# A hybrid decoder layer on one core: the experts' rows in slot order, loaded by plain transfers; four fp32 chunks per expert; a moved output norm

## The chip, the cores and the metric

The kernel runs on one core of a Trainium2 chip. The metric is the device time of one execution in microseconds. It was measured three times for the kernel before: median 2206.45 us, from 2205.89 to 2207.40. The profile below is of a further execution.

## The reference

One layer over 2048 tokens of width 1024, all fp32: a mixer (retention in four heads beside a gated short convolution), then a hierarchical mixture of 64 experts, then a last norm.

```python
def mixer(h, w_in, ret_gn_w, conv_w, w_o):
    proj = h @ w_in                                   # 1024 -> 3584
    ...
    return jnp.concatenate([ret, conv], axis=-1) @ w_o

def hier_moe(h, rg_w, rg_b, re_w, re_b, w_gate, w_up, w_down):
    ...
    p_group, g_sel = lax.top_k(g_prob, 1)             # one group of 8
    ...
    top_p, top_i = lax.top_k(e_prob, TOP_K)           # 2 of the group's 8 experts
    gate = p_group[:, None] * (top_p / jnp.sum(top_p, axis=-1, keepdims=True))
    # every token's row goes through its two experts:
    #   y += gate * (silu(x @ w_gate[e]) * (x @ w_up[e])) @ w_down[e]
    ...

x = x + mixer(rmsnorm(x, norm1_w), ...)
x = x + hier_moe(rmsnorm(x, norm2_w), ...)
return rmsnorm(x, final_norm_w)
```

An expert has 1024 x 512 weights for gate and for up and 512 x 1024 for down, 6 MB in fp32. A token's two experts belong to the same group. The kernel gives each expert 96 slots; what does not fit goes through a loop at the end, which these inputs don't need for more than a check of the count.

## The kernel before

**Dense stage.** The sequence goes in four blocks of 512 tokens. For each block the kernel projects the input (`w_in`), runs retention and convolution and projects back (`w_o`). Weight pieces come into the buffer `wraw` and are split by ScalarE and VectorE into a high and a low part, so that a product of fp32 accuracy is three fast matmuls (`hi hi`, `hi lo`, `lo hi`). A matmul on unsplit fp32 data is called an fp32 chunk here; it shows as two records of the same matmul. A table of steps (`at(step, function, ...)`) sets where the smaller work of a block stands between the matmuls.

**Routing.** For each tile of 128 tokens of a block: `turn_rows` adds the squares and takes the reciprocal root (GpSimd, `rr`, L455), and stores the residual rows to the output; `norm_rows` makes h and stores it to `h_rows` in the order of tokens; `logits`, `choose`, `rank1`, `rank2`, `gates` and `spread` (L592) find each token's experts, its rank among the expert's tokens and the entries of a table that holds for each expert and slot the token's number. `address` and `record` write the same entries to a list in memory by indirect stores from GpSimd (L573). In the last block the table is built on chip (`place`), since the first expert waits for it, and the tiles' routing goes one after another between the last matmuls of `w_o`.

**Experts.** `estream` lists the work: for each q the eight chunks of gate and the eight of up of expert q, then the eight steps of down of expert q-1 (`wi` is 0, 1, 2 for gate, up, down; `c` is the chunk). The pieces of that loop that matter here:

- `load_unit` (L631): SP loads weights in units of 1 MB, six to an expert, into 17 buffers, each as soon as its buffer's last reader is done. SP issues in program order. Each transfer also waits for the one eight before it: in the program's listing, `DMAHW0` to `DMAHW7` are the counters of SP's transfers in rotation, and `DMASW0` to `DMASW7` those of GpSimd's.
- `split_hi` (ScalarE, L671) and `split_lo` (VectorE, L677) split two chunks at once, a piece, LEAD = 5 pieces ahead of the matmuls. `plain(w, c)` (L656) names the chunks that are not split: two of eight of gate and of up, four of eight of down, eight per expert in all. So eight pieces per expert are split.
- `gather(q + 3)` (L698) at the first chunk of gate: GpSimd fetches the 96 rows of h of expert q+3 from `h_rows` by an indirect transfer; a slot without a token has an index out of bounds and moves nothing. `xpose` (L720 to L727) transposes them on TensorE and splits six of eight chunks into `xhi` and `xlo`; two remain whole.
- `regather(q + 1)` (L705) then fetches the rows of the residual stream, from the output in memory, into the same buffer. A buffer `row` or `pair` thus holds first h, then the residual row, to which `add_rows` adds the expert's weighted product.
- `hpose` (L751) transposes the hidden rows of expert q-1, which `up_act` has written as [k, p].
- For the experts of the later half of each token's pair (`later`), `norm1_rows` squares the finished rows in two halves (ScalarE) at chunk 4 of gate, `norm2_rows` scales them (L789, L792) at chunk 4 of up, and `put_rows` (L820) stores them to the output by an indirect transfer. The first eight experts are stored without the norm.

Before each indirect transfer GpSimd writes a `spacer`.

Of the kernel before, what the change touches and what calls it, by code (L numbers as in the profile page):

```python
# [79 lines left out]
def hybrid_layer(ctx: ExitStack, tc: tile.TileContext, x, xT, norm1, w_in, gn_w, conv_w, w_o, norm2, norm2r,  # L80
# [4 lines left out]
    h_d = nc.dram_tensor("h_rows", (S, D), F32, kind="Internal").ap()  # L85
    list_d = nc.dram_tensor("slots", (RANKS * NE, 4), F32, kind="Internal").ap()
# [386 lines left out]
    def norm_rows(b, i, eng, to=None):  # L473
        t = x2t[i]
        to = t if to is None else to
        r2 = rt["r2"][:, i:i + 1]
        if eng is dve:
            dve.scalar_tensor_tensor(to, t, r2, n2b, op0=OP.mult, op1=OP.mult)
        else:
            act.activation(to, t, AF.Copy, scale=r2)  # L480
            pool.tensor_tensor(to, to, n2b, op=OP.mult)
        r0 = b * C + i * P
        sp.dma_start(h_d[r0:r0 + P, :], to)

# [80 lines left out]
    def address(b, i):  # L565
        c = rt["c", i]
        dve.scalar_tensor_tensor(c["slot"], c["rk"], float(NE), c["e"], op0=OP.mult, op1=OP.add)

# [87 lines left out]
    def plain(w, c):  # L656
        return c >= (4 if w == 2 else 6)
# [34 lines left out]

    def gather(q):
        if q >= NE:
            return
        e = order[q]
        spaced()
# [12 lines left out]
    NX, NH = 6, 2  # L710


    def xpose(q):
        g, w = row_of(q), EX["work"]
        hi, lo = (w.tile([P, NX, CAP], F32R, name="x" + n) for n in ("hi", "lo"))
        whole = w.tile([P, KD - NX, CAP], F32, name="xwhole")
        for k0 in (0, 4):
            p = bank("pxg")
            for j in range(4):
                pe.transpose(p[:, j * P:j * P + CAP], g[:, k0 + j::KD], ident[:CAP, :CAP])  # L720
            pv = p.rearrange("p (k t) -> p k t", k=4)[:, :, :CAP]
            n = min(4, NX - k0)
            ks = slice(k0, k0 + n)
            act.activation(hi[:, ks], pv[:, :n], AF.Copy)  # L724
            dve.tensor_tensor(lo[:, ks], pv[:, :n], hi[:, ks].bitcast(F32), op=OP.subtract)  # L725
            if n < 4:
                act.activation(whole, pv[:, n:], AF.Copy)  # L727
        EX["xT", q] = hi, lo, whole
# [7 lines left out]
    def gate_act(q, p):  # L736
        sg = EX["work"].tile([CAP, FF], F32, name="sg")
# [3 lines left out]
    def up_act(q, p):  # L741
        h = EX["work"].tile([CAP, KF, P], F32, name="hrow")
        dve.tensor_tensor(h.rearrange("t k p -> t p k"), p.rearrange("t (p k) -> t p k", k=KF),
                          EX["sg", q].rearrange("t (p k) -> t p k", k=KF), op=OP.mult)
        EX["h", q] = h

    def hpose(q):
        w = EX["work"]
        p = bank("ph")
        for k in range(KF):  # L750
            pe.transpose(p[:, k * P:k * P + CAP], EX["h", q][:, k], ident[:CAP, :CAP])  # L751
# [3 lines left out]
        pv = p.rearrange("p (k t) -> p k t", k=KF)[:, :, :CAP]  # L755
        act.activation(hi, pv[:, :n], AF.Copy)
        dve.tensor_tensor(lo, pv[:, :n], hi.bitcast(F32), op=OP.subtract)
        act.activation(whole, pv[:, n:], AF.Copy)
# [8 lines left out]
    def add_rows(q, ys):  # L767
        r = row_of(q)
        EX["s", q] = EX["work"].tile([CAP, 3], F32, name="osum", bufs=2)
# [5 lines left out]
    def norm1_rows(q):  # L775
        e, sums, r = order[q], EX["s", q], row_of(q)
# [58 lines left out]
    at(12, prep_consts)  # L835
    for b in range(NB):
# [31 lines left out]
        if b < NB - 1:  # L868
# [5 lines left out]
            for i in range(TB):  # L874
# [7 lines left out]
                at(so + 2 * i + 7, address, b, i)  # L882
                at(so + 2 * i + 7, record, b, i)
# [45 lines left out]
    for m in range(TB):  # L929
        for n, s in enumerate(rest):  # L930
# [7 lines left out]
            else:  # L938
# [75 lines left out]
    dve.tensor_scalar(nsec, sec, -1.0, 1.0, op0=OP.mult, op1=OP.add)  # L1014
    for i in range(TB):
# [7 lines left out]
    for i, (q, wi, c) in enumerate(estream):  # L1023
# [7 lines left out]
        if i in (36, 40, 44):  # L1031
            two = pair(FIRST[i // 4 - 9])
            if i < 44:
                EX["rows"] += two
                for j in (2, 1):
                    clear(len(EX["rows"]) - j)
                    if i == 36:
                        gather(5 - j)
# [17 lines left out]
        if wi < 2:  # L1056
# [12 lines left out]
            if wi == 1 and c == 4 and later(q - 2):  # L1069
                norm2_rows(q - 2)  # L1070
                put_rows(q - 2)
            if c == 7:
# [4 lines left out]
                else:  # L1077
# [4 lines left out]
                    else:  # L1082
                        weights(q - 1)
                        weights(q, EX["fw"])
        else:
# [4 lines left out]
            if q < NE - 1:  # L1090
                if c == 7:
# [122 lines left out]
```

## Time and profile before

| | |
|---|---|
| median of 3 runs | 2206.45 us |
| the profiled execution's own time | 2207.35 us |
| its span (first to last instruction) | 2205.5 us |
| TensorE busy | 2154.6 us, 98% |
| VectorE busy | 1417.4 us, 64% |
| ScalarE busy | 1127.9 us, 51% |
| GpSimd busy | 768.8 us, 35% |
| mean DMA rate | 262 GB/s |

Shares of busy time are means over stages: up to about 930 us the dense stage runs, from 944 us on the experts. In the profile PE is TensorE, DVE VectorE, ACT ScalarE, POOL GpSimd and SP the engine that issues plain transfers. "DMA share" is the mean busy share of the core's 16 DMA engines, q1 the queue of plain transfers, q0 that of indirect ones. Matmul records overlap, so the pace of matmuls is read from their starts. A row of SP's timeline with xN stands for N issues one behind the other, from the first one's start to the last one's end, waits between them included.

### The profile page before, as it was taken

What the parts mean: (1) busy time and instruction counts of PE and PEld (TensorE: products, weight loads), DVE (VectorE), ACT (ScalarE), POOL (GpSimd) and SP (SyncE); (2) the same over time, 40 slices, a digit from 0 to 9 for tenths busy, and PEclk for the clock granted to TensorE, in tenths of its full rate; (3) what the DMA queues carried; (4) which work ended last, traced back from release to release, by engine and by line L of the source; (5) the groups of instructions that cost most, each with busy time, mean ns of one, the idle gap of its engine ahead of it and who ended that gap; (6) DMA issues with size and microseconds to landing.
All of it is one profiled execution on the core that took longest, in us unless ns stands there. A gap on an engine that the chain in (4) does not pass through costs nothing. (4 is left out here: it accounts for less than half of the span.)

```text
span 2205.5 us, 27810 instructions
## 1 busy us (share of the span) xinstructions
PE 2154.6 (98%) x9417; PEld 1505.9 (68%) x9418; DVE 1417.4 (64%) x2265; ACT 1127.9 (51%) x1927; POOL 768.8 (35%) x982
## 2 busy tenths in 40 slices
PE   8999999999999999799999999999999999999998
PEld 6888888888888888655656656656555555555554
DVE  4667566657566666666666666666666665666665
ACT  4324342443343323555556666666655665566564
POOL 0010031002200120331234444445555655565556
PEclk9999999999999999899999999999999999999999
DMA  8335344524453446679999999999999999999994
GB/s 263 108 112 177 95 141 129 167 92 153 123 164 96 134 155 241 229 247 370 363 360 361 360 364 359 353 352 363 357 354 347 356 354 354 358 357 358 357 359 154
DMA packets 136099, 578.69 MB, mean 262 GB/s; under 512 B 23440, under 2 KB 23792, under 8 KB 86736
## 3 DMA queue, kind: packets, MB, share of 16 engines
q1 hardware_dynamic: 113424, 526.43, 67.9%
q0 software_dynamic: 22528, 50.44, 7.2%
q8 instruction: 75, 1.23, 0.2%
q14 instruction: 72, 0.59, 0.1%
HBM read 559.94 MB, written 44.20 MB: 274 GB/s over the span
## 5 line engine op out<-in xcount | busy, mean ns | idle before, releaser
L677 DVE TENSOR_TENSOR ring<-unit,ring 128x1024 fp32r<-128x1024 f32 x342 | 411.7, 1230 | 230.7 <-ACT ring L671 225.3
L671 ACT ACTIVATE ring<-unit 128x1024 fp32r<-128x1024 f32 x342 | 346.0, 1051 | 190.6 <-DMA unit<-in_w_gate_dram 105.5
L291 PE MATMUL acc<-hhi,ring 128*128 128x512 f32 x1280 | 404.9, 393 | 8.5 <-ACT ring L166 5.6
L167 DVE TENSOR_TENSOR ring<-wraw,ring 128x512 fp32r<-128x512 f32 x256 | 172.6, 687 | 185.0 <-ACT ring L166 185.0
L166 ACT ACTIVATE ring<-wraw 128x512 fp32r<-128x512 f32 x256 | 153.7, 625 | 265.2 <-issue 111.0
L291 PEld LDWEIGHTS acc<-hhi,ring 128*128 128x128 f32 x1280 | 241.6, 189 | 58.3 <-ACT ring L166 5.3
L677 DVE TENSOR_TENSOR part<-unit,part 128x1024 fp32r<-128x1024 f32 x170 | 206.3, 1229 | 112.8 <-ACT part L671 111.5
L291 PE MATMUL acc<-hlo,ring 128*128 128x512 f32 x640 | 250.2, 391 | 0.0
L1052 PE MATMUL acc<-unit,xwhole 128*96 128x512 f32 x512 | 240.4, 592 | 0.0
L1052 PE MATMUL acc<-unit,ewhole 128*96 128x512 f32 x512 | 230.3, 592 | 0.0
L671 ACT ACTIVATE part<-unit 128x1024 fp32r<-128x1024 f32 x170 | 173.7, 1051 | 93.5 <-DMA unit<-in_w_gate_dram 50.4
L732 PE MATMUL acc<-ring,xhi 128*96 128x512 f32 x512 | 217.5, 425 | 2.7 <-ACT xhi L724 2.4
L734 PE MATMUL acc<-ring,xlo 128*96 128x512 f32 x512 | 202.9, 396 | 7.1 <-DVE xlo L725 7.1
L733 PE MATMUL acc<-ring,xhi 128*96 128x512 f32 x512 | 202.5, 396 | 0.0
L291 PE MATMUL acc<-ring,mix 128*128 128x512 f32 x768 | 185.4, 396 | 0.0
L291 PE MATMUL acc<-ring,hhi 128*128 128x512 f32 x512 | 162.2, 398 | 0.0
L291 PEld LDWEIGHTS acc<-ring,mix 128*128 128x128 f32 x768 | 142.6, 189 | 28.6
L1052 PEld LDWEIGHTS acc<-unit,ewhole 128*96 128x96 f32 x512 | 83.3, 163 | 110.7 <-issue 101.6
L764 POOL TENSOR_SCALAR pair<-pair,sec,nsec 96x1024 f32<-96x1024 f32 x56 | 147.3, 2630 | 2.6
L1052 PEld LDWEIGHTS acc<-unit,xwhole 128*96 128x96 f32 x512 | 83.1, 162 | 86.1 <-issue 68.1
L792 POOL TENSOR_TENSOR pair<-pair 96x1024 f32<-96x1024 f32 x31 | 77.9, 2513 | 182.3 <-ACT pair L789 182.2
L291 PEld LDWEIGHTS acc<-hlo,ring 128*128 128x128 f32 x640 | 121.1, 189 | 24.2
(233 smaller groups left out, 3641.8 us busy)
## 6 DMA issues: line engine op xcount, KB each, us to landing
unit<-in_w_down_dram SPq DMA_DIRECT2D x128, 1024.0 KB
unit<-in_w_gate_dram SPq DMA_DIRECT2D x128, 1024.0 KB
unit<-in_w_up_dram SPq DMA_DIRECT2D x128, 1024.0 KB
wraw<-in_w_in_dram SPq DMA_DIRECT2D x225, 256.0 KB
wraw<-in_w_o_dram SPq DMA_DIRECT2D x64, 256.0 KB
xs<-in_x_dram SPq DMA_DIRECT2D x16, 512.0 KB
x<-in_x_dram SPq DMA_DIRECT2D x16, 512.0 KB
out_dram<-x SPq DMA_DIRECT2D x16, 512.0 KB
```

What stands on the lines that cost most here:

```text
L166: act.activation(hi, src, AF.Copy)
L167: dve.tensor_tensor(lo, src, hi.bitcast(F32), op=OP.subtract)
L291: pe.matmul(o, l, r, start=first and j == 0, stop=last and j == 2)
L671: act.activation(t[:, 0], src, AF.Copy)
L677: dve.tensor_tensor(lo, src, hi.bitcast(F32), op=OP.subtract)
L732: pe.matmul(o, ahi, whi, start=first, stop=False)
L733: pe.matmul(o, ahi, wlo, start=False, stop=False)
L734: pe.matmul(o, alo, whi, start=False, stop=last)
L764: pool.tensor_scalar(m, EX["fw"], EX["sec"][:, e:e + 1], EX["nsec"][:, e:e + 1], op0=OP.mult, op1=OP.add)
L792: pool.tensor_tensor(r, r, m, op=OP.mult)
L1052: pe.matmul(o, whole[:, k - hi.shape[1]], wt, start=False, stop=last)
```

## The change

1. **Rows in slot order.** A second array `h_slots` holds h in the order of expert and slot, 64 x 96 rows. 48 plain transfers fill it with zeros during the dense stage (`fill_slots`). For each tile, `sort_rows` writes its 128 rows of h there by two indirect stores from GpSimd (each token has two experts); `address` computes the slots on VectorE. From expert 3 on `gather` is one plain transfer of 96 rows, issued by SP; `clear` of those row buffers is dropped.
2. **Four fp32 chunks.** `plain` is now true only for the last four steps of w_down. All chunks of gate and up are split, ten pieces per expert, and `xpose` splits all eight chunks of x.
3. **Hidden rows.** `up_act` writes h as it comes; the transposes read it with a stride.
4. **Output norm.** `norm1_rows` squares all 1024 columns at once, so the GpSimd addition goes; `norm2_rows` and `put_rows` move from chunk 4 of up of expert q to chunk 4 of down of expert q-1, eight chunks later.

```diff
+    hs_d = nc.dram_tensor("h_slots", (NE * CAP, D), F32, kind="Internal").ap()
...
+    def fill_slots(i):
+        sp.dma_start(hs_d[i * P:(i + 1) * P], empty[:P * D // 4].rearrange("(p n) w -> p (n w)", p=P))
...
     def address(b, i):
...
+        dve.tensor_scalar(far, c["rk"], float(CAP), float(NONE), op0=OP.is_ge, op1=OP.mult)
+        dve.tensor_tensor(far, far, c["rk"], op=OP.add)
+        dve.scalar_tensor_tensor(hs, c["e"], float(CAP), far, op0=OP.mult, op1=OP.add)
...
+    def sort_rows(b, i):
+        c = rt["c", i]
+        for j in range(2):
+            pool.memset(spacer, 0.0)
+            s_ = pool.indirect_dma_start(
+                out=hs_d, out_offset=bass.IndirectOffsetOnAxis(ap=c["hslot"][:, j:j + 1], axis=0),
+                in_=c["h"], in_offset=None, bounds_check=NE * CAP - 1, oob_is_err=False)
...
     def plain(w, c):
-        return c >= (4 if w == 2 else 6)
+        return w == 2 and c >= 4
...
     def gather(q):
...
+        if q >= 3:
+            sp.dma_start(row_of(q), hs_d[e * CAP:(e + 1) * CAP])
+            return
...
     def norm1_rows(q):
...
-        for half in range(2):
-            junk = EX["work"].tile([CAP, 512], BF16, name="ojunk")
-            act.activation(junk, r[:, half * 512:half * 512 + 512], AF.Square, accum_out=sums[:, half:half + 1])
...
-        pool.tensor_tensor(ss, sums[:, 0:1], sums[:, 1:2], op=OP.add)
+        junk = EX["work"].tile([CAP, D], BF16, name="ojunk2", tag="sg")
+        act.activation(junk, r, AF.Square, accum_out=ss)
...
+    for i in range(NFILL):
+        at(20 + 3 * i // 2, fill_slots, i)
...
+                at(so + 2 * i + 7, sort_rows, b, i)
...
                         address(b, m - 1)
+                        sort_rows(b, m - 1)
...
+    for i in (2, 3):
+        sort_rows(b, i)
...
-            if wi == 1 and c == 4 and later(q - 2):
-                norm2_rows(q - 2)
-                put_rows(q - 2)
...
+                if c == 4 and later(q - 1):
+                    norm2_rows(q - 1)
+                    put_rows(q - 1)
```

Three places in the order of the instructions show what this moves. The first is GpSimd in the last block's routing, between one tile's `spread` and the next tile's `rr`. `what` is the product of `spread`, `wraw` holds the tile's rows of h. Before:

```order
L459 COPY rec<-cons 128x2x2
L481 TENSOR_TENSOR wraw<-wraw,n2b 128x1024 [waits DMAHW2_49,DMAHW0_49,DMAHW4_49,DVE_49,Activation_49]
L592 TENSOR_TENSOR what<-full,rec 128x128 [waits DVE_49,Pool_49]
L592 TENSOR_TENSOR what<-full,rec 128x256 [waits DVE_49]
L455 TENSOR_TENSOR rr_7286<-rss 128x1 [waits Activation_49]
L217 TENSOR_SCALAR rr_7286<-rr_7286 128x1 [waits Pool_49]
L218 TENSOR_TENSOR rr_7286<-rr_7286,cons 128x1 [waits Pool_49]
```

After, with lines shifted by the added code:

```order
L619 TENSOR_TENSOR what<-full,rec 128x128 [waits DVE_49,Pool_49]
L619 TENSOR_TENSOR what<-full,rec 128x256 [waits DVE_49]
L588 MEMSET spacer 1x1
L589 DMA h_slots<-wraw,hslot 6144x1024 [waits DMASW0_49,DVE_49,Pool_49]
L588 MEMSET spacer 1x1 [waits Pool_49]
L589 DMA h_slots<-wraw,hslot 6144x1024 [waits DMASW1_49]
L462 TENSOR_TENSOR rr_7490<-rss 128x1 [waits Activation_49]
L224 TENSOR_SCALAR rr_7490<-rr_7490 128x1 [waits Pool_49]
L225 TENSOR_TENSOR rr_7490<-rr_7490,cons 128x1 [waits Pool_49]
```

Two spacers and two stores to `h_slots` now stand between `spread` and `rr`; it is so for tiles 0 and 1 of this block.

The second is SP in the expert stage, one expert's loads. Before:

```order
L631 DMA unit<-in_w_gate_dram 128x2048 [waits DMAHW5_49,DVE_49]
L631 DMA unit<-in_w_gate_dram 128x2048 [waits DMAHW6_49,PE_49]
L631 DMA unit<-in_w_up_dram 128x2048 [waits DMAHW7_49,DVE_49]
L631 DMA unit<-in_w_up_dram 128x2048 [waits DMAHW0_49,DVE_49,PE_49]
L631 DMA unit<-in_w_down_dram 128x2048 [waits DMAHW1_49,DVE_49]
L631 DMA unit<-in_w_down_dram 128x2048 [waits DMAHW2_49,DVE_49,PE_49]
```

After:

```order
L658 DMA unit<-in_w_gate_dram 128x2048 [waits DMAHW0_49,DVE_49]
L658 DMA unit<-in_w_gate_dram 128x2048 [waits DMAHW1_49,PE_49]
L726 DMA row_8066<-h_slots 96x1024 [waits DMAHW2_49,DMASW5_49,Pool_49]
L658 DMA unit<-in_w_up_dram 128x2048 [waits DMAHW3_49,DVE_49]
L658 DMA unit<-in_w_up_dram 128x2048 [waits DMAHW4_49,DVE_49]
L658 DMA unit<-in_w_down_dram 128x2048 [waits DMAHW5_49,DVE_49]
L658 DMA unit<-in_w_down_dram 128x2048 [waits DMAHW6_49,DVE_49]
```

The load of `row` from `h_slots` stands behind the two w_gate loads, and waits for a store of GpSimd's that last used the buffer.

The third is SP at the end of the dense stage, where a weight load takes over the buffer `wraw` that held h of the last block. Before:

```order
L483 DMA h_rows<-wraw 128x1024 [waits DMAHW4_49,Pool_49]
L463 DMA out_dram<-x_1_97 128x1024 [waits DMAHW5_49,DVE_49]
L483 DMA h_rows<-wraw 128x1024 [waits DMAHW6_49,Pool_49]
L631 DMA unit<-in_w_gate_dram 128x2048 [waits DMAHW7_49,PE_49]
L631 DMA unit<-in_w_up_dram 128x2048 [waits DMAHW4_49,DMAHW6_49,DMAHW0_49,Activation_49]
L631 DMA unit<-in_w_gate_dram 128x2048 [waits DMAHW1_49,DVE_49]
```

After:

```order
L490 DMA h_rows<-wraw 128x1024 [waits DMAHW4_49,Pool_49]
L470 DMA out_dram<-x_1_97 128x1024 [waits DMAHW5_49,DVE_49]
L490 DMA h_rows<-wraw 128x1024 [waits DMAHW6_49,Pool_49]
L658 DMA unit<-in_w_gate_dram 128x2048 [waits DMAHW7_49,PE_49]
L658 DMA unit<-in_w_up_dram 128x2048 [waits DMASW3_49,DMAHW0_49,DMASW2_49,DMAHW4_49,DMASW1_49,DMAHW6_49,DMASW0_49,Activation_49]
L658 DMA unit<-in_w_gate_dram 128x2048 [waits DMAHW1_49,DVE_49]
L658 DMA unit<-in_w_up_dram 128x2048 [waits DMAHW2_49,DVE_49,Activation_49]
```

The load of w_up behind the first w_gate load now also waits for four of GpSimd's transfers, among them the stores of tiles 2 and 3, and the loads behind it stand behind that wait.

## Rows read from the trace of the kernel before

**Rows 1.** Stages: stretch, length, busy (xcount) per engine, PEclk, DMA share, GB/s

```profile
100.00:850.00 750.00, 750.00 (x3773) 632.00 (x3772) 481.50 (x1110) 280.21 (x588) 114.54 (x214) 1.00 0.42 134
...
950.00:1000.00 50.00, 49.80 (x199) 30.01 (x198) 34.66 (x38) 30.20 (x41) 17.56 (x27) 1.00 0.83 286
1000.00:1400.00 400.00, 400.00 (x1586) 240.61 (x1584) 271.95 (x292) 243.12 (x363) 152.24 (x210) 1.00 1.00 363
1400.00:2150.00 750.00, 737.20 (x2890) 436.00 (x2888) 479.51 (x529) 463.61 (x718) 418.71 (x448) 1.00 1.00 355
```

**Rows 2.** SP's timeline, early experts: start, length, engine, line, transfer

```profile
1144.21 6.98 SPq L631 DMA_DIRECT2D unit<-in_w_gate_dram  x2
...
1163.39 6.98 SPq L631 DMA_DIRECT2D unit<-in_w_gate_dram  x2
```

**Rows 3.** SP's timeline, late experts

```profile
1803.32 5.41 SPq L631 DMA_DIRECT2D unit<-in_w_up_dram  x2
...
1823.35 5.69 SPq L631 DMA_DIRECT2D unit<-in_w_up_dram  x2
```

**Rows 4.** ScalarE's waits, 1400 to 2150 us: total, times, longest

```profile
ACT ring L671 <- DMA unit<-in_w_gate_dram: 104.1, 43, 3.7
```

**Rows 5.** SP's timeline, last loads

```profile
2087.88 0.33 SPq L631 DMA_DIRECT2D unit<-in_w_up_dram  x1
...
2130.22 2.83 SPq L631 DMA_DIRECT2D unit<-in_w_down_dram  x2
2136.17 3.15 SPq L631 DMA_DIRECT2D unit<-in_w_gate_dram  x2
2143.50 3.22 SPq L631 DMA_DIRECT2D unit<-in_w_up_dram  x2
2148.87 8.13 SPq L631 DMA_DIRECT2D unit<-in_w_down_dram  x4
```

**Rows 6.** Stretches of 4 us after the last loads

```profile
2162.00:2166.00 4.00, 4.00 (x22) 2.92 (x21) 3.04 (x3) 2.60 (x4) 3.92 (x2) 1.00 0.77 302
...
2178.00:2182.00 4.00, 4.00 (x16) 2.23 (x15) 2.58 (x4) 2.30 (x3) 3.71 (x4) 1.00 0.10 43
```

**Rows 7.** GpSimd's timeline, a late expert

```profile
1813.24 1.04 POOL L820 DMA_INDIRECT out_dram<-row,ix  x1 [0.25 <-POOL spacer L691]
```

**Rows 8.** DMA queues, 1200 to 2100 us: packets, MB, share

```profile
q0 software_dynamic: 15265, 35.30, 12.0%
```

**Rows 9.** DMA queues, 200 to 220 us

```profile
q1 hardware_dynamic: 1440, 3.15, 48.5%
```

**Rows 10.** DMA queues, 220 to 240 us

```profile
q1 hardware_dynamic: 998, 1.83, 29.4%
```

**Rows 11.** TensorE's timeline, last expert

```profile
2173.04 0.39 PE L732 MATMUL acc<-ring,xhi 128*96 128x512 f32 x1
...
2173.73 1.88 PE L1052 MATMUL acc<-unit,xwhole 128*96 128x512 f32 x4
2175.45 0.49 PE L751 MATMUL ph<-cons,hrow 96*128 96x96 f32 x4
```

**Rows 12.** VectorE's groups by line: xcount, busy us, mean ns, idle before

```profile
L677 DVE TENSOR_TENSOR ring<-unit,ring 128x1024 fp32r<-128x1024 f32 x342 | 411.7, 1230 | 230.7 <-ACT ring L671 225.3 <-DMA unit<-in_w_up_dram 4.0 <-ACT xwhole L727 1.3
```

**Rows 13.** GpSimd's timeline, routing of the last block

```profile
905.13 0.62 POOL L592 TENSOR_TENSOR what<-full,rec 128x256 f32<-128x256 bf16 x1 [2.91 <-DVE slot L567]
905.70 0.19 POOL L455 TENSOR_TENSOR rr<-rss 128x1 f32<-128x1 f32 x1
...
947.22 0.98 POOL L573 DMA_INDIRECT slots<-rec,slot  x1 [0.22 <-issue]
...
948.50 0.96 POOL L573 DMA_INDIRECT slots<-rec,slot  x1 [0.22 <-issue]
...
949.76 2.00 POOL L573 DMA_INDIRECT slots<-rec,slot  x1 [0.21 <-issue]
```

**Rows 14.** A stretch of 10 us at the first expert

```profile
940.00:950.00 10.00, 7.41 (x28) 5.35 (x29) 5.76 (x13) 4.22 (x6) 4.75 (x9) 0.63 0.31 82
```

More of the change, by code (lines that the diff above doesn't have):

```diff
@@ L483, in norm_rows @@
         sp.dma_start(h_d[r0:r0 + P, :], to)
+        rt["c", i]["h"] = to
     def logits(i, half):
@@ L567, in address @@
         dve.scalar_tensor_tensor(c["slot"], c["rk"], float(NE), c["e"], op0=OP.mult, op1=OP.add)
+        far, hs = small([2], "far"), small([2], "hslot", I32, bufs=2, pool=base)
+        dve.tensor_scalar(far, c["rk"], float(CAP), float(NONE), op0=OP.is_ge, op1=OP.mult)
+        dve.tensor_tensor(far, far, c["rk"], op=OP.add)
+        dve.scalar_tensor_tensor(hs, c["e"], float(CAP), far, op0=OP.mult, op1=OP.add)
+        c["hslot"] = hs
+    row_writes = []
+    def sort_rows(b, i):
[5 more added lines that the diff above has]
+                in_=c["h"], in_offset=None, bounds_check=NE * CAP - 1, oob_is_err=False)
+            for o_ in row_writes:
+                tc.declare_no_dep(s_.ins, o_.ins, reason="different slots")
+            row_writes.append(s_)
     def record(b, i):
@@ L608, in count_blocks @@
         pe.matmul(p[:, :NE], ones, cums[:, 0], start=True, stop=True)
-        f, n = (EX["work"].tile([P, NE], t, name="cnt" + k) for k, t in (("f", F32), ("n", I32)))
+        f, n = (EX["work"].tile([P, NE], t, name="cnt" + k, tag=tag) for k, t, tag in (("f", F32, "sg"), ("n", I32, "hrow")))
         dve.tensor_scalar(f, p[:, :NE], float(-CAP), 0.0, op0=OP.add, op1=OP.max)
@@ L708, in regather @@
         moved("g", q, i)
-    NX, NH = 6, 2
+    NH = 2
     def xpose(q):
         g, w = row_of(q), EX["work"]
-        hi, lo = (w.tile([P, NX, CAP], F32R, name="x" + n) for n in ("hi", "lo"))
-        whole = w.tile([P, KD - NX, CAP], F32, name="xwhole")
-        for k0 in (0, 4):
+        hi, lo = (w.tile([P, KD, CAP], F32R, name="x" + n) for n in ("hi", "lo"))
+        for half in range(2):
             p = bank("pxg")
             for j in range(4):
-                pe.transpose(p[:, j * P:j * P + CAP], g[:, k0 + j::KD], ident[:CAP, :CAP])
+                pe.transpose(p[:, j * P:j * P + CAP], g[:, half * 4 + j::KD], ident[:CAP, :CAP])
             pv = p.rearrange("p (k t) -> p k t", k=4)[:, :, :CAP]
[L722 to L728, printed above, removed]
+            ks = slice(half * 4, half * 4 + 4)
+            act.activation(hi[:, ks], pv, AF.Copy)
+            dve.tensor_tensor(lo[:, ks], pv, hi[:, ks].bitcast(F32), op=OP.subtract)
+        EX["xT", q] = hi, lo, None
     def mm3(o, ahi, alo, w, first, last):
@@ L736, in gate_act @@
     def gate_act(q, p):
-        sg = EX["work"].tile([CAP, FF], F32, name="sg")
+        sg = EX["work"].tile([CAP, FF], F32, name="sg", tag="sg")
         act.activation(sg, p, AF.Silu)
@@ L741, in up_act @@
     def up_act(q, p):
-        h = EX["work"].tile([CAP, KF, P], F32, name="hrow")
-        dve.tensor_tensor(h.rearrange("t k p -> t p k"), p.rearrange("t (p k) -> t p k", k=KF),
-                          EX["sg", q].rearrange("t (p k) -> t p k", k=KF), op=OP.mult)
+        h = EX["work"].tile([CAP, FF], F32, name="hrow")
+        dve.tensor_tensor(h, p, EX["sg", q], op=OP.mult)
         EX["h", q] = h
@@ L775, in norm1_rows @@
     def norm1_rows(q):
[L776 to L779 removed]
+        e, r = order[q], row_of(q)
         ss = EX["work"].tile([CAP, 1], F32, name="oss", bufs=2)
[L781 removed]
+        junk = EX["work"].tile([CAP, D], BF16, name="ojunk2", tag="sg")
+        act.activation(junk, r, AF.Square, accum_out=ss)
         rms(ss, ss, 1)
@@ L1034, in hybrid_layer @@
                 EX["rows"] += two
[L1035 to L1038, printed above, removed]
+                if i == 36:
+                    for j in (3, 4):
+                        gather(j)
             else:
@@ L1090, in hybrid_layer @@
             if q < NE - 1:
+                if c == 4 and later(q - 1):
+                    norm2_rows(q - 1)
+                    put_rows(q - 1)
+                    if q == NE - 2:
+                        weights(q)
+                        weights(q + 1, EX["fw"])
                 if c == 7:
```

9 lines of the change are left out of this document (3 added, 6 removed).

## The prediction, on record before the result was known

> **What bounds the kernel now.** I read the busy time by stage first. From 100 to 850 us (input projection, retention, output projection) TensorE is busy without a break and the DMA engines 42% of the time; from 1000 us on the 64 experts run, and there both TensorE and the DMA engines show as full [rows 1]. Two full resources can't both set the pace, so the next view is SP's queue, which issues the 1 MB weight loads, six to an expert. Early on, one expert follows another every 1163.39 - 1144.21 = 19.18 us, the same for one expert after another [rows 2]. Late it is 1823.35 - 1803.32 = 20.03 us [rows 3]. Then ScalarE's waits: between 1400 and 2150 us its splits of weights wait 104.1 us for the w_gate loads to land [rows 4], and TensorE loses 13 us of busy time [rows 1]. So the first experts are paced by TensorE, which uses up weights loaded ahead, and the later ones by the loads.
>
> What limits the loads is not their sum. After the last four loads are issued, from 2148.87 on and 8.13 us long [rows 5], the DMA share does not stay at 1.00 and then drop: it is 0.77 at 2162 to 2166 us and still 0.10 at 2178 to 2182 [rows 6]. A load is spread over 16 engines, so some of them finish these loads long after the others. SP's order shows that each transfer waits for the one eight before it to land, so the latest engine sets the pace. Where no indirect traffic is near, one load follows the other after 2.50 us: two w_down issues from 2130.22 on take 2.83 us together, and one issue by itself takes 0.33 [rows 5]. Six make 15.0 us. The other 5.03 us of the 20.03 come with the three indirect transfers that GpSimd issues for each expert one behind the other, the store of finished rows (the first, at 1813.24 [rows 7]), the re-read of x and the gather of h. They have 96 slots, but 900 us hold 45 experts of 20.03 us, so 135 of these transfers, and 35.30 MB [rows 8] are 64 rows of 4 KB for each. My reading, which no row shows engine by engine, is that empty slots stand at the end of the list, so the engines with the first slots carry all rows and are the late ones.
>
> **The change part by part.**
>
> *The gather.* Before, on the late engines, three transfers cost 5.03 us, a third is 1.68 us. The other price: at the end no gather is left (it runs three experts ahead). From 2130.22 to 2148.87 six loads are issued in 18.65 us [rows 5]; six times 2.50 are 15.0, so store and re-read cost 3.65 us, which leaves 5.03 - 3.65 = 1.38 us for a gather. If the store cost nothing, the gather would be 2.5 us. After, a plain load of 96 rows of 4 KB gives every engine 6 rows. A plain row of 4 KB: in 220 to 240 us queue q1 takes 29.4% of 16 x 20 us = 94.1 us for 1.83 MB in 2 KB packets, 0.105 us each [rows 10]; in 200 to 220 us it takes 155.2 us for 1024 of those (107.8 us) and 256 of 4 KB, 0.185 us each [rows 9]. Six are 1.11 us. Saved on the late engine: 1.68 - 1.11 = 0.57 us per expert, between 0 (a plain row costs in the crowd what a gathered one does) and 1.4. I take 0.57, by thirds, since the price at the end was read with emptier queues. The DMA share is 1.00 from 1000 to 2162 us, 1162 / 20.03 = 58 experts: **-33 us**. GpSimd also loses a memset and an issue, and it waits for others anyway: nothing. The load now stands in SP's queue behind the weights, lands about eight transfers later, and is wanted 2.7 experts after its issue: nothing. It waits for the row's store, which was issued more than an expert earlier; if that were late, the weight loads behind it on SP would be held.
>
> *Fewer fp32 chunks.* TensorE: three split matmuls take 2173.73 - 2173.04 = 0.69 us, an fp32 chunk, which has two records, (2175.45 - 2173.73) / 2 = 0.86 us [rows 11]. Four chunks change, 0.17 us each: 0.7 us per expert. Where the loads set the pace this is worth nothing; it lowers TensorE's own pace to 18.5 us, and once, behind the last load, it counts: **-0.7 us**. In return VectorE does two more splits of 1.23 us [rows 12], ScalarE two too. VectorE was busy 479.5 of 750 us, 12.8 us per expert [rows 1]; with 2.5 us more it is some 15.3 of 19.5 us (the longer `lo` of x and the shorter product for h are small beside that and of opposite sign). That hides, if no chain forms (rival).
>
> *Sorted rows, dense stage.* 48 fills of 512 KB and 24 stores of 512 KB for the first three blocks go beside TensorE. The cover is a DMA share of 0.42 [rows 1]; if all 37.7 MB came at 355 GB/s on top it would be 106 us of DMA spread over 750: nothing.
>
> *Sorted rows, last block.* Here it costs. In the last block the routing of one tile follows the other on GpSimd: `spread` at 905.13 for 0.62 us, then at 905.70, at once, `rr` of the next tile [rows 13], which gives VectorE the scale for that tile's logits. Tiles 0 and 1 now have two scatters and two memsets between these two. A scatter with its memset takes 948.50 - 947.22 = 1.28 us; one took 2.00 us by itself, 2.3 with the memset and the gap [rows 13]. 2 x 2 x 1.28 = **+5.1 us**, up to 4 x 2.3 = 9.2, before the first expert starts, when the DMA engines are nearly idle (0.31 at 940 to 950 us [rows 14]), so nothing takes it back. The scatters of tiles 2 and 3 come after the first re-read of x, and hold on SP the weight load that takes their buffer, and one behind it. Those two loads, 5 us, then fall into a stage with a share of 0.83 [rows 1], 50 x 0.17 = 8.5 us free: nothing, +5 us if that room is gone.
>
> *Output norm.* One square of 1024 for two of 512 saves a read-out and a GpSimd add; scaling and store come eight chunks later, long before the row is reused. In the last experts GpSimd scales itself and keeps its order: nothing.
>
> **The sum**, against the profiled execution's own 2207.35 us: -33 - 0.7 + 5.1 = 2178.8 us. It stands 0.9 us above the median of the runs, so 2178 us.
>
> **The rivals.**
>
> 1. *A plain row costs what a gathered one did.* Saved 0 per expert; the routing chain's 5.1 us decides alone: 2206.45 + 5.1 - 0.7 = 2211 us, slower. It decides where a plain gather takes over 1.68 - 5/58 = 1.6 us on the late engine. For it: all 16 engines get six rows, where the empty ones had none. Against: 0.185 us per row with queue q1 lightly loaded. Chance 0.13.
>
> 2. *The sum of all engines is the limit.* From expert 3 on the gather moves 32 empty rows more: 61 x 32 x 4 KB = 8.0 MB, at 355 GB/s 22.5 us: 2206.45 + 22.5 + 5.1 - 0.7 = 2233 us. For it: the steady 363 and 355 GB/s [rows 1]. Against: the uneven end [rows 6]. Chance 0.09. [...]
>
> 3. *More relief: TensorE becomes the bound.* If gather and re-read carry all of the 5.03 us, the loads fall below TensorE's 18.5 us. Then 23 experts that ran at 19.18 save 0.7 and 38 that ran at 20.03 save 1.5: 73 us, less 5.1: 2138 us. Chance 0.13.
>
> 4. *VectorE and ScalarE form a chain.* Ten pieces per expert instead of eight run only five ahead, in gate and up one every 1.4 us for 1.23 us of VectorE. With half of the relief lost, 2195 us. Chance 0.13, of which a quarter ends without a gain.
>
> **How the numbers follow.** The forecast, 2165 to 2192 us, has 0.52. The range goes from rival 3's 2138 us to rival 1's with the dearer scatters, 2211 + 4 = 2215 us; it leaves out rival 2 and what lies below rival 3. About 0.2%, 4.4 us, is what a measurement of this kernel can tell from no change. Faster: 0.52 + 0.13 + 0.10 = 0.75. Slower: 0.13 x 0.9 + 0.09 = 0.20. Same: 0.05.
>
> **What would show it.** In the new profile SP's queue in the late stage should repeat every 19.3 to 19.6 us per expert, with seven transfers; the share after the last load should fall faster; the first expert should start 5 us later than before; GpSimd should show two scatters between `spread` and `rr`. A late pace of 20 us or more with ScalarE still waiting for loads speaks for rivals 1 or 2, which the drain at the end tells apart; a pace of 18.5 us for rival 3; a pace between with VectorE over 90% busy for rival 4. I would be wrong in kind if the dense stage lost TensorE time, or SP stood at a plain gather for a row's store.

## The result: 4.0% slower

The changed kernel takes 2294.4 us (median of 4 runs, 2287.6 to 2301.7), the kernel before 2206.2 us in the same comparison: a ratio of 1.0397, with a 95% interval from 1.038 to 1.0413. I had forecast 2178 us and a range up to 2215. The profiled execution, the fastest of the four, has a span of 2285.8 us, 80.3 us more than before.

The stages after the change, as in [rows 1] (stretch, length, busy time per engine, clock, DMA share, GB/s):

```profile
100.00:850.00 750.00, 747.27 (x3757) 628.79 (x3756) 482.78 (x1135) 278.20 (x586) 139.60 (x262) 1.00 0.54 178
...
950.00:1000.00 50.00, 48.77 (x214) 32.79 (x213) 42.96 (x51) 34.08 (x41) 26.53 (x32) 1.00 0.94 337
1000.00:1400.00 400.00, 383.99 (x1631) 249.99 (x1629) 318.25 (x323) 263.27 (x340) 157.80 (x142) 1.00 1.01 350
1400.00:2150.00 750.00, 681.81 (x2815) 432.55 (x2814) 572.51 (x562) 479.82 (x633) 382.21 (x319) 0.99 1.00 340
```

TensorE, which was busy 737.2 of 750 us in the late expert stage [rows 1], is now busy 681.8. The DMA share is 1.00 as before, but the engines move 340 GB/s instead of 355. SP's queue in the late stage, for [rows 3]:

```profile
1806.66 3.01 SPq L658 DMA_DIRECT2D unit<-in_w_gate_dram  x2
1812.74 0.33 SPq L726 DMA_DIRECT2D pair<-h_slots  x1
1814.25 3.66 SPq L658 DMA_DIRECT2D unit<-in_w_up_dram  x2
1822.28 3.40 SPq L658 DMA_DIRECT2D unit<-in_w_down_dram  x2
1828.26 3.92 SPq L658 DMA_DIRECT2D unit<-in_w_gate_dram  x2
1834.44 0.33 SPq L726 DMA_DIRECT2D pair<-h_slots  x1
```

From one plain gather to the next are 1834.44 - 1812.74 = 21.70 us, where an expert took 20.03 us before. The gathers themselves don't hold SP: each is issued in 0.33 us and the next load follows within 2 us. Who waits is ScalarE; its splits into `ring` now wait for w_gate and w_up together 156.4 us, where w_gate alone was 104.1 [rows 4]:

```profile
ACT ring L698 <- DMA unit<-in_w_gate_dram: 85.4, 41, 4.8
ACT ring L698 <- DMA unit<-in_w_up_dram: 71.0, 27, 4.8
```

The end of the dense stage, for [rows 13]: the stores of sorted rows stand between `spread` and `rr`, as the order had shown, and the re-read of expert 1's rows (L736) comes late.

```profile
905.41 0.62 POOL L619 TENSOR_TENSOR what<-full,rec 128x256 f32<-128x256 bf16 x1 [2.91 <-DVE rec L549]
905.97 0.09 POOL L588 MEMSET spacer<- 1x1 f32 x1
907.03 1.11 POOL L589 DMA_INDIRECT h_slots<-wraw,hslot  x1 [0.97 <-POOL spacer L588]
...
908.44 0.97 POOL L589 DMA_INDIRECT h_slots<-wraw,hslot  x1 [0.21 <-issue]
909.42 0.22 POOL L462 TENSOR_TENSOR rr<-rss 128x1 f32<-128x1 f32 x1
...
973.21 2.04 POOL L736 DMA_INDIRECT row<-out_dram,ix  x1 [0.23 <-issue]
```

From `spread` to `rr` are 4.01 us instead of 0.57, so two tiles cost 6.9 us. The re-read of expert 1's rows was issued at 958.68 before:

```profile
958.68 0.99 POOL L705 DMA_INDIRECT row<-out_dram,ix  x1 [0.78 <-PE pxg L720]
```

SP stands there too. Its load of w_up that waits for the sorting stores of tiles 2 and 3 was issued 931.67 - 929.14 = 2.5 us after the w_gate load ahead of it, and is now issued 959.02 - 936.22 = 22.8 us after it, behind the last of those stores; the loads behind it stand as long. Before:

```profile
929.14 0.38 SPq L631 DMA_DIRECT2D unit<-in_w_gate_dram  x1
931.67 0.33 SPq L631 DMA_DIRECT2D unit<-in_w_up_dram  x1
```

After:

```profile
936.22 0.38 SPq L658 DMA_DIRECT2D unit<-in_w_gate_dram  x1
954.37 2.02 POOL L589 DMA_INDIRECT h_slots<-wraw,hslot  x1 [0.23 <-issue]
959.02 0.33 SPq L658 DMA_DIRECT2D unit<-in_w_up_dram  x1
```

The first expert's first matmul (`acc<-ring,xhi`) starts at 948.36 instead of 944.09, 4.3 us later.

### The profile page after: what moved, and what is told of

Its sections match the earlier page's. It is cut to its first block, busy times and chain, and to the rows that moved or that the text cites. A ratio compares the mean times of both kernels' runs of the same rounds, so it can differ in the third digit from the quotient of the medians.

```text
span 2285.8 us, 28475 instructions
## 1 busy us (share of the span) xinstructions
PE 2146.8 (94%) x9673; PEld 1556.4 (68%) x9674; DVE 1631.2 (71%) x2441; ACT 1218.6 (53%) x1877; POOL 813.9 (36%) x869
## 5 line engine op out<-in xcount | busy, mean ns | idle before, releaser
L704 DVE TENSOR_TENSOR ring<-unit,ring 128x1024 fp32r<-128x1024 f32 x428 | 565.9, 1343 | 179.0 <-ACT ring L698 178.1
L698 ACT ACTIVATE ring<-unit 128x1024 fp32r<-128x1024 f32 x428 | 442.8, 1054 | 297.4 <-DMA unit<-in_w_gate_dram 122.7
L704 DVE TENSOR_TENSOR part<-unit,part 128x1024 fp32r<-128x1024 f32 x212 | 281.7, 1343 | 92.8 <-ACT part L698 92.1
L760 PE MATMUL acc<-ring,xlo 128*96 128x512 f32 x684 | 276.6, 404 | 29.7 <-DVE xlo L753 29.7
L698 ACT ACTIVATE part<-unit 128x1024 fp32r<-128x1024 f32 x212 | 220.2, 1053 | 149.3 <-DMA unit<-in_w_gate_dram 59.3
L759 PE MATMUL acc<-ring,xhi 128*96 128x512 f32 x684 | 273.8, 400 | 24.3 <-DVE ring L704 24.2
L758 PE MATMUL acc<-ring,xhi 128*96 128x512 f32 x684 | 286.4, 419 | 9.2 <-ACT xhi L752 9.0
L760 PEld LDWEIGHTS acc<-ring,xlo 128*96 128x96 f32 x684 | 111.9, 164 | 89.3 <-DVE xlo L753 45.4
L759 PEld LDWEIGHTS acc<-ring,xhi 128*96 128x96 f32 x684 | 112.3, 164 | 86.4 <-DVE ring L704 38.8
L758 PEld LDWEIGHTS acc<-ring,xhi 128*96 128x96 f32 x684 | 113.9, 166 | 68.9 <-ACT xhi L752 26.1
L789 POOL TENSOR_SCALAR pair<-pair,sec,nsec 96x1024 f32<-96x1024 f32 x56 | 159.1, 2841 | 2.7
```

Of the source, the lines that this page charges most:

```text
L698: act.activation(t[:, 0], src, AF.Copy)
L704: dve.tensor_tensor(lo, src, hi.bitcast(F32), op=OP.subtract)
L758: pe.matmul(o, ahi, whi, start=first, stop=False)
L759: pe.matmul(o, ahi, wlo, start=False, stop=False)
L760: pe.matmul(o, alo, whi, start=False, stop=last)
L789: pool.tensor_scalar(m, EX["fw"], EX["sec"][:, e:e + 1], EX["nsec"][:, e:e + 1], op0=OP.mult, op1=OP.add)
```

## The experiments

Theory A: the plain gathers alone make the kernel slower. Theory B: the extra splits form a chain of ScalarE and VectorE. Theory C: the fills and sorting stores disturb the rest. All ratios below are against the kernel before, measured beside each run (2207 to 2208 us).

### Which part of the change costs

**e1: parts 2 to 4 alone.** The changed kernel without `fill_slots`, `sort_rows`, the extra lines of `address` and the plain branch:

```diff
-        if q >= 3:
-            sp.dma_start(row_of(q), hs_d[e * CAP:(e + 1) * CAP])
-            return
```

> Parts 2 to 4 of the change alone (four fp32 chunks, hidden rows, output norm); the rows come by indirect gathers from token order as before, and nothing is sorted. Theory A, the plain gather is what costs: the loads still pace the experts at 20.0 us, so 2206 us less at most a few, 2195 to 2210. Theory B, the extra splits form a chain of ScalarE and VectorE: 2260 us or more, with TensorE waiting for splits whose weights have long landed.

2202.2 us, ratio 0.9975 (0.9963 to 0.9986). Early experts follow each other after 1173.42 - 1154.76 = 18.66 us; before it was 19.18 [rows 2]. SP's queue:

```profile
1154.76 10.01 SPq L653 DMA_DIRECT2D unit<-in_w_gate_dram  x2
...
1173.42 10.01 SPq L653 DMA_DIRECT2D unit<-in_w_gate_dram  x2
```

So the four fp32 chunks give TensorE 0.52 us per expert, and no chain of splits takes it back. Theory B is out.

**e2: part 1 alone**, on the kernel before: `hs_d`, `fill_slots`, `sort_rows` with its calls, the lines of `address` and the plain branch, as in the diff of the change.

> Part 1 of the change alone, on the kernel before: sorted rows and plain gathers, with eight fp32 chunks and the old output norm. Theory A: nearly the whole loss, 2280 to 2300 us, with 21.3 us or more per expert in SP's queue. Theory B: only the 7 us of the longer routing, about 2213 us.

2298.4 us, ratio 1.0396 (1.036 to 1.0432): all of the loss.

**e3: the gathers back.** Only the three lines of e1's diff are taken out (and `clear` is back); fills and sorting stores stay.

> The changed kernel with one thing undone: rows of all experts come by GpSimd's indirect gather from token order; the fills and the sorting stores stay, though nobody reads what they write. Theory A: the time of parts 2 to 4 alone plus some 7 us of routing, 2203 to 2217 us. If the fills and sorting stores were the cost (theory C), it would stay near 2290 us.

2215.6 us, ratio 1.0039 (1.0024 to 1.0054). With e1 this splits the change into terms: parts 2 to 4 give 2202.2 - 2207.3 = -5.1 us, sorting costs 2215.6 - 2202.2 = 13.4 us, and the step from indirect to plain gathers costs 2294.4 - 2215.6 = 78.8 us, 1.3 us for each of 61 experts. Theory A holds, C accounts for the 13.4.

### Was the reading of before right?

**e4: the kernel before with spread slots.** Rank r of an expert's tokens sits at position (r mod 16) x 6 + r / 16, in the table built on chip and in the list:

```diff
-            dve.tensor_tensor(c["here"], bc(iota[:, None, :CAP], [2, CAP]), bc(rk[:, :, None], [2, CAP]), op=OP.is_equal)
+            for j in range(2):
+                dve.tensor_scalar(c["here"][:, j].rearrange("p (b a) -> p b a", b=16),
+                                  iota[:, :CAP].rearrange("p (a b) -> p b a", b=16), rk[:, j:j + 1], None, op0=OP.is_equal)
...
-        sp.dma_start(t, list_d[:CAP * NE].rearrange("(s e) r -> s e r", e=NE))
+        for k in range(6):
+            sp.dma_start(t[k::6], list_d[:CAP * NE].rearrange("(k b e) r -> k b e r", k=6, e=NE)[k])
```

> The kernel before with one change: rank r of an expert's tokens sits at position (r mod 16) x 6 + r / 16, so that the empty slots spread evenly over the 96. It moves the same rows and bytes. If each DMA engine moves six neighbouring slots and the engine with the fullest slots sets the pace (my reading of the trace before), the late engine has 4 rows of a transfer instead of 6: a third of 5.03 us, 18.4 us per expert for the loads, and TensorE's 19.2 us sets the pace: 2206 - 38 x 0.85 = 2174 us, between 2160 and 2185. If the sum of all engines is the limit, or rows are dealt to the engines one by one: 2206 us within 5.

2184.1 us, ratio 0.989 (0.9869 to 0.9911). The late stage, and one expert in SP's queue:

```profile
1400.00:2150.00 750.00, 750.00 (x2973) 451.78 (x2972) 513.43 (x548) 483.34 (x741) 351.56 (x464) 1.00 0.99 362
```

```profile
1815.63 6.98 SPq L634 DMA_DIRECT2D unit<-in_w_gate_dram  x2
...
1834.81 6.99 SPq L634 DMA_DIRECT2D unit<-in_w_gate_dram  x2
```

TensorE is busy all 750 us, and the late pace is the early one, 1834.81 - 1815.63 = 19.18 us. The same rows and bytes, put elsewhere in the list, remove the limit: the place of the empty slots was what paced the late experts. The gain is 23 us where I had reckoned 32. That the engines with the full slots were the late ones fits, but no view names an engine. Nor is it all that the edit changed: queue q1, which carries the weights alone here, needs 44.6 us of its engines' time for one MB before and 42.5 in e4 (share x 16 x 600 us by MB, from 1500 to 2100 us; packets, MB, share):

```profile
q1 hardware_dynamic: 25989, 189.24, 88.0%
```

```profile
q1 hardware_dynamic: 26990, 196.60, 87.0%
```

So slower weight packets may have had a part in the limit too; that isn't settled.

**e5: e1 and e4 together,** by their two diffs.

> Parts 2 to 4 together with the evenly spread slots of the run before, no sorted rows. With the slots spread the loads no longer set the pace, and TensorE needs 0.7 us less per expert through the four fp32 chunks that are now split: 2184 - 61 x 0.7 = 2141 us, 18.5 us per expert. If the loads take over between 18.5 and 19.2 us: 2150 to 2184.

2151.5 us, ratio 0.9748 (0.9731 to 0.9764): the first run over 2% faster than the kernel before. It is 10 us above the first forecast, as the four chunks give TensorE 0.52 us per expert (e1) and not 0.7. TensorE is busy throughout, at 379 GB/s:

```profile
1400.00:2100.00 700.00, 700.00 (x2998) 463.07 (x2997) 572.62 (x600) 521.14 (x674) 526.56 (x410) 1.00 1.01 379
```

### What a plain gather costs

**e6: the changed kernel with spread slots**, the sorted rows too: e4's diff, and in `address`

```diff
+        dve.tensor_scalar(pos, c["rk"], 16.0, None, op0=OP.is_ge)
+        for k in range(2, 6):
+            dve.scalar_tensor_tensor(pos, c["rk"], 16.0 * k, pos, op0=OP.is_ge, op1=OP.add)
+        dve.scalar_tensor_tensor(far, pos, -95.0, far, op0=OP.mult, op1=OP.add)
+        dve.scalar_tensor_tensor(far, c["rk"], 5.0, far, op0=OP.mult, op1=OP.add)
```

> The changed kernel with evenly spread slots (the sorted rows too). Store and re-read now put 4 rows each on every engine instead of 6 on the late ones; the plain gather stays 6 on every engine. Theory A1, rows on the late engine are what counts: 15.0 + 2.4 + 2/3 x 3.7 = 19.9 us instead of 21.3 per expert, about 2210 us, between 2195 and 2230. Theory A2, the sum of all transfers limits the plain gathers: no gain, 2280 to 2300.

2272.5 us, ratio 1.0281 (1.0256 to 1.0306), and SP's queue still shows 1839.01 - 1817.22 = 21.79 us per expert late:

```profile
1817.22 0.33 SPq L735 DMA_DIRECT2D pair<-h_slots  x1
...
1839.01 0.33 SPq L735 DMA_DIRECT2D pair<-h_slots  x1
```

Only 22 us come back, neither theory's number. The profile is of the slowest of the four executions (2290.7 us, the others 2264.8 to 2276.2), but its late pace is no better than the 21.70 us after the change: with plain gathers the uneven stores and re-reads are not the main limit of the late experts.

**e7: each plain gather in two transfers of 48 rows.**

```diff
-            sp.dma_start(row_of(q), hs_d[e * CAP:(e + 1) * CAP])
+            for r in (0, 48):
+                sp.dma_start(row_of(q)[r:r + 48], hs_d[e * CAP + r:e * CAP + r + 48])
```

> The changed kernel with each plain gather issued as two of 48 rows: the same rows and bytes, one transfer more per expert in SP's queue. Theory A1: no change, 2294 us within 10. Theory A3, a plain gather costs because it takes one of the eight places that SP's transfers have in flight, in which else a 1 MB load would stand: another place per expert is lost, 2340 us or more.

2308.1 us, ratio 1.0469 (1.0424 to 1.0514): 14 us more, over the 10 that theory A1 allowed, and a third of what the theory of lost places asked for. Neither holds as it stands.

**e8: no plain gathers.** `gather` returns at once from expert 3 on, and the transposes read the constant tile `fw` instead of the experts' rows.

```diff
-            sp.dma_start(row_of(q), hs_d[e * CAP:(e + 1) * CAP])
             return
...
-        g, w = row_of(q), EX["work"]
+        g, w = row_of(q) if q < 3 else EX["fw"], EX["work"]
```

> The changed kernel with the plain gathers left out (from expert 3 on the experts work on one constant tile instead of their rows); all else stays, fills and sorting stores too. It gives the price of the plain gathers, against the changed kernel, and of the indirect ones, against the run with the gathers back (2215.6 us). By the 2.4 us that a plain gather seems to hold the latest engine: 18.9 us per expert or TensorE's 18.5, so 2145 to 2165 us. By the price in my prediction, 1.1 us: 2230 us.

2158.6 us, ratio 0.9773 (0.9753 to 0.9793), with TensorE busy all the time:

```profile
1000.00:1400.00 400.00, 400.00 (x1713) 264.70 (x1712) 340.56 (x343) 284.74 (x363) 176.42 (x155) 1.00 0.97 367
1400.00:2100.00 700.00, 700.00 (x3012) 465.25 (x3011) 613.00 (x604) 524.28 (x679) 405.19 (x337) 1.00 0.97 367
```

A plain gather costs at least (2294.4 - 2158.6) / 61 = 2.2 us, an indirect one at least (2215.6 - 2158.6) / 61 = 0.9 us; at least, since TensorE's pace hides the first part of each.

**e9, e10, e11, e14, e17: loads that nobody reads**, put into e8, where the experts work on the constant tile. Theory G here is that what counts is whether a load covers all 128 partitions. The load is one line each; in e11 and e17 the row buffers also get 128 partitions:

```diff
+            sp.dma_start(row_of(q)[:64], hs_d[e * CAP:e * CAP + 64])                  # e9
+            sp.dma_start(row_of(q), h_d[t0:t0 + CAP])                                 # e10
+            sp.dma_start(EX["full"][q % NROW], hs_d[t0:t0 + P])                       # e11, P = 128
+            sp.dma_start(row_of(q)[:64].rearrange("s (h w) -> s h w", h=2)[:, :, :480], ...)  # e14
+            sp.dma_start(EX["full"][q % NROW][:, :512], hs_d[t0:t0 + P, :512])        # e17
```

> The run without plain gathers (2158.6 us; the experts work on one constant tile), with a plain load of the first 64 rows of the expert put back in their place, read by nobody: 4 rows for every engine instead of 6. The full 96 rows cost 2294.4 - 2158.6 = 136 us. Theory D, it is the rows: two thirds of the price or less (TensorE's pace hides the first part), 2200 to 2250 us. Theory E, it is one more transfer in SP's queue, whatever its size: 2280 to 2300 us.

> As the run before this, with 96 rows in one piece from the array in token order, which the indirect gathers read, instead of the one in slot order. Theory D: 2294 us within 12, the source is no matter. Theory F, the array in slot order is slow to read (where it lies, or how it was written): 2160 to 2220 us.

> [...] Theory D: a third more rows, 136 x 4/3 or more, 2335 to 2350 us. [...]

> As the run with 64 rows that nobody reads (2301.7 us), but each row in two pieces of 1.9 KB (480 of 512 columns), so 128 pieces, eight for every engine, on 64 partitions. [...] Theory G2, a transfer of SP's queue runs well when it has 128 pieces, like a weight load: 2160 to 2190 us.

> As the run with 64 rows of 4 KB that nobody reads (2301.7 us), with the same bytes as 128 half rows of 2 KB on 128 partitions. Theory G: cheap, 2155 to 2180 us. If bytes or the number of transfers were the price: 2290 us or more.

| run | partitions x bytes | KB | time, us | ratio (interval) |
|---|---|---|---|---|
| e8 | none | 0 | 2158.6 | 0.9773 (0.9753 to 0.9793) |
| e9 | 64 x 4096 | 256 | 2301.7 | 1.0426 (1.0401 to 1.045) |
| e14 | 64 x 2 x 1920 | 240 | 2302.1 | 1.0442 (1.0411 to 1.0473) |
| e10 | 96 x 4096, other source | 384 | 2297.5 | 1.0408 (1.0373 to 1.0442) |
| e17 | 128 x 2048 | 256 | 2158.5 | 0.9782 (0.976 to 0.9804) |
| e11 | 128 x 4096 | 512 | 2177.7 | 0.9872 (0.985 to 0.9895) |

64 rows cost as much as 96, and 128 rows a seventh of it. The same 256 KB are free on 128 partitions and cost 143 us on 64. Neither rows (D), nor the number of transfers (E), nor the source (F), nor the number of pieces (G2) is the price: it is that the load covers 64 or 96 partitions and not 128. The views of SP's queue q1 between 1500 and 2100 us (packets, MB, share of the 16 engines' time) show where it goes. After, e8, e9, e11, e17:

```profile
q1 hardware_dynamic: 27594, 188.97, 92.2%
```

```profile
q1 hardware_dynamic: 27803, 202.46, 88.6%
```

```profile
q1 hardware_dynamic: 26410, 183.34, 91.9%
```

```profile
q1 hardware_dynamic: 31328, 211.79, 92.7%
```

```profile
q1 hardware_dynamic: 32241, 210.43, 91.0%
```

Share x 16 x 600 us by MB is the engine time for one MB: 46.8 us after the change and 48.1 in e9, but 42.0 in e8, 42.0 in e11 and 41.5 in e17. In the packet records of these traces a weight packet (8 KB) takes 377 ns on the mean after the change and 386 in e9, but 343 in e8, 342 in e11 and 338 in e17. A packet of the rows (4 KB) takes 234 and 273 ns after the change and in e9, and 178 in e11. So a partial load makes the weight packets slow too, not only its own.

Why a load of 64 or 96 partitions is dear and slows the weight packets is not shown: no view names the engine of a packet, nor the partition that it goes to.

**e12 and e15: another queue.** The complete changed kernel, its 96-row loads issued by GpSimd or by ScalarE:

```diff
-            sp.dma_start(row_of(q), hs_d[e * CAP:(e + 1) * CAP])
+            pool.dma_start(row_of(q), hs_d[e * CAP:(e + 1) * CAP])      # e12
+            act.dma_start(row_of(q), hs_d[e * CAP:(e + 1) * CAP])       # e15
```

> The changed kernel with its plain gathers issued from GpSimd's queue instead of SP's, behind the same waits; the same 96 rows. Theory D: 2294 us within 15. Theory H, a row costs more in SP's queue because it stands in one line with the weights on each engine, while a row in GpSimd's queue is taken in between: towards the run with the indirect gathers (2215.6 us) plus the price of 32 rows more, 2220 to 2255 us.

> The changed kernel with its plain gathers of 96 rows issued from ScalarE's queue instead of SP's. Theory H, rows are cheap as soon as they don't stand in one line with the weights: 2215 to 2255 us, as from GpSimd's queue (2217.7). If what made them cheap there is GpSimd's way of issuing: 2285 to 2305 us. [...]

e12: 2217.7 us, ratio 1.0049 (1.0024 to 1.0074), the time of the indirect gathers. e15: 2229.7 us, ratio 1.0092 (1.0073 to 1.0111). The rows of e15 have a queue of their own, q10:

```profile
q1 hardware_dynamic: 25948, 188.97, 86.4%
q0 software_dynamic: 6720, 15.59, 7.7%
q10 hardware_dynamic: 3311, 11.60, 6.3%
```

So the same load costs less where it doesn't stand in line with the weights: q1 needs 43.9 us for one MB here. Theory H had forecast 2220 to 2255 and 2215 to 2255 us, so e15 is inside and e12 2 us below, and it holds beside G; why another queue is cheaper isn't shown.

The 12 us between e15 and e12 lie ahead of the experts. `sg` is ScalarE's first step on an expert's product of gate, once per expert (shortest, median and longest in ns, then first and last start in us). In e12 and in e15:

```profile
L764 ACT ACTIVATE sg<-acc x64: 565/575/595, 957.0 to 2186.0; 96x512 f32<-96x512 f32 x64
```

```profile
L764 ACT ACTIVATE sg<-acc x64: 570/575/595, 970.5 to 2198.4; 96x512 f32<-96x512 f32 x64
```

From the first to the last are 1229.0 us in e12 and 1227.9 in e15, so among the experts the two queues cost the same, and GpSimd's own way of issuing adds nothing. The profiled executions of e6, e13, e14, e15 and e18 all start their first `sg` late, between 968.0 and 977.6 us; in the other runs that sort it stands between 955.2 and 958.5. The edits of e14 and e15 don't touch what runs ahead of it, so the reason is open.

### Mending the change

**e13: 128 rows.** The changed kernel, complete, with loads of 128 rows (the row buffers have 128 partitions, `h_slots` and the fills 128 rows more):

```diff
-            sp.dma_start(row_of(q), hs_d[e * CAP:(e + 1) * CAP])
+            sp.dma_start(EX["full"][q % NROW], hs_d[e * CAP:e * CAP + P])
```

> [...] From the run with 128 rows that nobody read (2177.7 us): 2178 us, between 2168 and 2190. If that run was fast because its experts didn't wait for their rows: 2270 us or more.

2179.4 us, ratio 0.9868 (0.985 to 0.9887). A third more bytes, 115 us less. The late stage now runs at 383 GB/s:

```profile
1000.00:1400.00 400.00, 400.00 (x1723) 266.09 (x1722) 341.94 (x346) 286.54 (x367) 153.06 (x152) 1.00 1.00 391
1400.00:2100.00 700.00, 695.37 (x2970) 458.00 (x2969) 601.72 (x591) 510.57 (x666) 381.01 (x333) 1.00 1.01 383
```

**e18: e13 with spread slots,** by the diffs of e13 and e6.

> The changed kernel with plain gathers of 128 rows and, beside that, evenly spread slots. The loads then need less than TensorE, which sets the pace with 18.7 us per expert as in the run of 2151.5 us; what is left is the price of sorting, 2215.6 - 2202.2 = 13.4 us: 2165 us, between 2155 and 2175. If the late engine still paces: 2175 to 2185 us.

2174.6 us, ratio 0.9854 (0.9834 to 0.9875). The loads no longer pace anything, at 395 GB/s:

```profile
950.00:1000.00 50.00, 39.62 (x162) 26.73 (x163) 43.43 (x94) 32.17 (x44) 26.37 (x38) 0.79 0.77 289
1000.00:1400.00 400.00, 400.00 (x1722) 265.93 (x1721) 341.09 (x344) 285.56 (x365) 153.90 (x153) 1.00 1.00 393
1400.00:2100.00 700.00, 700.00 (x3005) 464.22 (x3004) 611.41 (x603) 521.62 (x674) 367.08 (x337) 1.00 1.01 395
```

The 23 us to e5 lie ahead of the experts. In e5 and in e18:

```profile
L759 ACT ACTIVATE sg<-acc x64: 572/573/596, 949.6 to 2119.3; 96x512 f32<-96x512 f32 x64
```

```profile
L773 ACT ACTIVATE sg<-acc x64: 569/577/596, 973.6 to 2142.0; 96x512 f32<-96x512 f32 x64
```

The experts take the same time, 1168.4 us in e18 and 1169.7 in e5, but the first starts 24.0 us later, and with sorted rows alone (e3) it starts at 958.1. `address` also computes the spread position here, but e13, which doesn't, starts late too (968.0), so that can't be all of it; this is the late start named under e15.

**e16: e5 with two fp32 chunks** instead of four.

```diff
-        return w == 2 and c >= 4
+        return w == 2 and c >= 6
...
-    NH = 2
+    NH = 3
```

> The fastest kernel so far (parts 2 to 4 with spread slots, 2151.5 us) with two more chunks of w_down split, two fp32 chunks left: TensorE 2 x 0.17 us less per expert, 2151.5 - 61 x 0.35 = 2130 us. If VectorE, with 1.3 us more per expert, begins to pace: 2150 us or more.

2138.5 us, ratio 0.9692 (0.9673 to 0.9711), the fastest of all:

```profile
1400.00:2100.00 700.00, 698.03 (x3131) 482.90 (x3130) 672.82 (x646) 562.57 (x725) 595.92 (x413) 1.00 1.01 377
```

VectorE is now busy 672.8 of 700 us, but it doesn't pace the experts:

```profile
L759 ACT ACTIVATE sg<-acc x64: 571/577/597, 951.4 to 2100.5; 96x512 f32<-96x512 f32 x64
```

From the first `sg` to the last are 1149.1 us, 20.6 less than in e5: 0.33 us for each of the 63 steps, where 0.35 was forecast. The 8 us that the run is short of its forecast lie elsewhere: the first `sg` starts 1.8 us later than in e5, and behind the last one the span goes on for 36.7 us instead of 30.1. Why the end grew wasn't settled.

## Why the prediction was wrong

**What bounds the kernel** was read rightly as far as e4 shows: the place of the empty slots paced the late experts, not the sum of all. That it did so through uneven engines alone is not shown.

**The gather's term failed**, and the whole result with it. "A plain row of 4 KB ... 0.185 us each" came from [rows 9], where the 4 KB packets belong to loads of 128 rows, the form that e11 shows to be cheap. I used it for a load of 96 partitions. The lower bound, 0 saved ("a plain row costs in the crowd what a gathered one does"), allowed no loss at all, and no row spoke for that bound. Nor did I ask what the new load does to the weight packets behind it in the same queue. Instead of -33 us the term is +78.8. The packet records show both parts. A row takes 234 ns in the weights' queue, not 185, so six, 96 by 16 engines, are 1.4 us instead of 1.11. And the 48 weight packets of an expert on the mean engine, 768 by 16, take 377 ns where they took 343 without the load (e8): 1.6 us, which the prediction put at nothing. Together they make some 3.0 us per expert, an estimate for the mean engine; the 2.2 us of e8 are what TensorE's pace doesn't hide of them.

**Fewer fp32 chunks:** 0.52 us per expert for TensorE instead of 0.7, and -5.1 us in e1 for parts 2 to 4 together instead of -0.7: a little relief comes through although the loads pace.

**Sorted rows, last block:** 6.9 us on GpSimd's chain instead of 5.1, since 1.06 us pass between the spacer and the first store of a tile; 4.3 us of them reach the first expert. The stores of tiles 2 and 3, costed at "nothing, +5 us if that room is gone", hold GpSimd's queue, where the re-read at 973.21 was at 958.68 before, and SP's, where the load of w_up comes 22.8 us behind the one ahead of it instead of 2.5. Sorting costs 13.4 us in all; how they divide is not shown. **Dense stage:** 747.3 of 750 us busy, so 2.7 us lost where I had put nothing; lost TensorE time there was one of my own signs of being wrong in kind.

**The output norm** shows no price of its own: it is within the -5.1 us.

**The rivals.** Rival 1 had the sign and its threshold, over 1.6 us, was passed; but its time, 2211 us, let the plain row cost no more than a gathered one, and that capped the range. Rival 2, a limit on the bytes of all, is out: e18 holds 395 GB/s for 700 us, where the 355 of [rows 1] had stood for such a limit. Rival 3's mechanism, TensorE as the bound, is what e5 and e18 show. Rival 4 is out with e1.

The measured terms, -5.1 + 13.4 + 78.8, make 87.1 us; the whole change measures 2294.4 - 2207.3 = 87.1, as it must, since they are steps from one kernel to the other. e2 is the independent test: part 1 alone costs 91 us.

## What to carry to other kernels

By these runs: take a transfer's price from a row with the same partitions, not only the same packet size (a 4 KB packet took 234 ns in a load of 96, 178 in one of 128), and let the bound for an unknown price include a loss to the transfers beside it. Load 128 partitions even where 96 are needed (2179.4 us instead of 2294.4), or keep partial loads out of the queue that carries the bulk (2217.7 and 2229.7). Where lists have empty ends, deal the full slots evenly before making transfers cheaper: that alone was worth 23 us.

## What the runs showed of the hardware

- A plain load of 64 partitions in the weights' queue cost 143 us over 61 loads, one of 128 partitions with the same bytes nothing (e9, e17).
- Beside loads of 96 partitions in their queue the weights' 8 KB packets took 377 ns on the mean, beside loads of 128 partitions 342 (after the change, e11).
- With the same 96-row loads the kernel took 2294.4 us from SP's queue, 2229.7 from ScalarE's and 2217.7 from GpSimd's; the last two differ ahead of the experts alone.
- A DMA share of 1.00 is by itself no sign of a limit: it stood at 340 GB/s after the change, and 1.01 at 379 in e5 and at 395 in e18, where TensorE set the pace.
